# Fixing TensorE's order of products in an encoder block, gating by one Silu, and moving its transfers to another queue

## The chip, the cores and the metric

The kernel runs on one core of a Trainium2 chip. The metric is the device time of one execution in microseconds (us). The engines of a core run side by side, each with its own queue of instructions in a fixed order: TensorE (PE; its weight loads are listed apart as PEld), VectorE (DVE), ScalarE (ACT), GpSimd (POOL) and SyncE (SP). SP computes nothing here; it issues transfers. POOL issues transfers too. An instruction at the head of a queue that waits holds up everything behind it on that engine.

## The reference

One layer of a bidirectional encoder on 1024 positions of width 1024, in float32:

```python
proj = x @ w_in                      # 5920 columns, cut into the parts below
# attention: 3 groups of 4 heads, windows (128,1), (512,4), (2048,16) = (width, dilation)
s = q @ k * dh**-0.5 + bias;  e = exp(s - max(s));  o = (e @ v) / sum(e)
y_attn = sum over groups of softmax(log denominators) * o
# gated linear attention, forward and backward scan, 4 heads of 64 x 128
y_gla = rmsnorm(o_fwd + o_bwd) * gla_norm_g * silu(gout)
merged = sigmoid(gate_a) * (y_attn @ w_attn_branch) + sigmoid(gate_g) * (y_gla @ w_gla_branch)
x = layernorm(alpha * x + merged @ w_out)
x = layernorm(alpha * x + square(relu(x @ w_ff1 + b_ff1)) @ w_ff2 + b_ff2)
```

Here silu(g) is g times sigmoid(g). The change bears on the input projection, on `silu(gout)` and on the attention that runs beside the projection.

## The kernel before

**Products.** Each float32 operand is split in two halves, hi and lo (a cast on ACT, a subtraction on DVE; `halve`, line 152), and a product is made of three matmuls, hi by hi, hi by lo and lo by hi (`mm3`, line 98). A block product of four 128-row slices is thus 12 matmuls of 512 columns.

**The projection by seven products.** Two blocks of 128 columns of `w_in` are computed together by a scheme of the Strassen kind (`proj`, line 638). The weight is cut in quarters A11, A12, A22 and sums S1 to S4, and x in quarters B11 to B22 and sums T1 to T4. The text orders the products m1, m6, m2, m7, m5, m4, m3. After each comes a sum on DVE (`add`, line 632): after m6 the sum u2 is updated; after m7 the function `u3` reads bank W and u2; after m5 `c22` reads bank Z. Product m4 then accumulates *onto bank W*, so it cannot start before `u3` has read it, and m3 accumulates onto bank Z after `c22`. In the order of the text m5 stands between m7 and m4. For the first ten pairs after the first two, m1 and m2 were partly made earlier (`kept`), and five products remain: m6, m7, m5, m4, m3.

**Steps.** The projection is a list of 98 steps (list `steps`, loop at line 1151). Steps 0 to 9 finish the first two pairs, steps 10 to 19 are the products of the attention's values (`v_do`, line 1063, each 24 matmuls of 384 columns; prepared by `v_prep`), steps 20 to 69 ten pairs of five products, steps 70 to 97 four pairs of seven. A step's operands are prepared three steps ahead. Beside the steps run "units": from step 35 on the 24 attention tiles (`visit`, line 1092), with scores, exponentials, transposes and the products with the values; and from step 8 on eight pieces of the gating.

**What sets the order.** The order of the text is not the order of the queues. A planner simulates the program and, for each engine, may take a later instruction that it holds to be ready before an earlier one that it holds to be waiting. `tc.issue_after(i)`, and `behind(k)` that looks `i` up under the name k (line 635), forbid this: the instructions inside are queued after instruction i of the same engine. The matmuls of a projection product stand behind the name "small" only, the last attention matmul; those of the values' products stand behind nothing. Products may so be exchanged among themselves. The first matmul of an attention tile's products with the values stands behind "pe", the last product. SP's transfers of weights, stored blocks and parked sums are chained by the name "sp", and POOL's by "pool" (`pool_dma`, line 826), which makes the order of these queues that of the text.

**Gating.** `silu(h, hf)` (line 1012) loads a piece g of gout and a piece y of the linear attention's output (both SP, lines 1018 and 1019), makes the sigmoid of g on ACT (line 1023), two multiplications on DVE (lines 1025 and 1026) and stores y (SP, line 1027). Two sets of buffers serve in turn. The loads of piece i are placed at step 8 + 2i, its work at step 12 + 2i.

**Statistics of the attention.** Groups 1 and 2 store each tile's minima and denominators (`smdr`); `stats(g)` (line 991) fetches them, in two transfers by POOL, at visits 12 and 16.

**The end of the stage.** From step 92 on `fed` (line 1136) loads the gating's and the attention's results and splits them for the merge, two pieces a step, ahead of the preparation of the projection's own operands.

Of the kernel before, what the change touches and what calls it, by code (L numbers as in the profile page):

```python
# [12 lines left out]
AF = mybir.ActivationFunctionType  # L13
OP = mybir.AluOpType
# [34 lines left out]
def turns(tiles, n):  # L49

    count = itertools.count()
    return lambda: tiles[next(count) % n]
# [20 lines left out]
def build(tc, io):  # L73
    nc = tc.nc
    V, G, A, T, SP = nc.vector, nc.gpsimd, nc.scalar, nc.tensor, nc.sync
    P = Pools(tc)
    issued = {}
# [10 lines left out]
    def load_w(src, shape, raw=None):  # L88
        if raw is None:
            raw = wp.tile(shape, F32, tag="raw", bufs=2, name="raw")  # L90
            issued["raw"] = SP.dma_start(raw, src)
        hi = wp.tile(shape, F32R, tag="whi", bufs=4, name="whi")
        A.copy(hi, raw)
        lo = wp.tile(shape, F32R, tag="wlo", bufs=4, name="wlo")
        V.tensor_tensor(lo, raw, hi.bitcast(F32), op=OP.subtract)
        return hi, lo

    def mm3(ps, pairs, first=True, last=True, more=False):

        n = len(pairs)  # L100
        for i, (lh, ll, rh, rl) in enumerate(pairs):
            T.matmul(ps, lh, rh, start=first and i == 0, stop=False, skip_group_check=more)  # L102
            T.matmul(ps, lh, rl, start=False, stop=False, skip_group_check=more)  # L103
            issued["pe"] = T.matmul(ps, ll, rh, start=False, stop=last and i == n - 1, skip_group_check=more)  # L104
# [4 lines left out]
    spill = dr.tile([36, 128, S], F32, name="spill")  # L109
    yodr = dr.tile([4, 128, S], F32, name="yodr")  # L110
    ygdr = dr.tile([4, 128, S], F32, name="ygdr")
# [3 lines left out]
    smdr = dr.tile([2, S, 8], F32, name="smdr")  # L115
# [73 lines left out]
    for k in range(KT):  # L189
        n = {0: 1, 1: 1, 2: 2, 4: 2, 6: 2}.get(k)  # L190
# [11 lines left out]
        for nm, hf in (("q", 0), ("k", 0), ("q", 1), ("k", 1)):  # L202
            hi, lo = w0[nm]
            sl = slice(hf * 512, hf * 512 + 512)
# [117 lines left out]
    for i in range(2):  # L322
        sl = slice(i * 512, i * 512 + 512)
# [186 lines left out]
    def xside(nm, p, k):  # L510
        return XQ[nm][:, p, k] if nm in XQ else XQ[nm, k][:, p]
# [120 lines left out]
    def add(o, a, b):  # L632
        issued["add"] = V.tensor_tensor(o, a, b, op=OP.add)  # L633

    def behind(k):
        return tc.issue_after(issued[k].ins) if k in issued else nullcontext()

    def proj(blocks, r, ahead, banks, kept=None):

        st, c, ps = {}, {}, {}  # L640

        def mm(b, l, x, more=False):
            if not more:
                ps[b] = banks()
            l = l.rearrange("p h (k f) -> p h k f", f=128)
            with behind("small"):
                mm3(ps[b], [(l[:, 0, k], l[:, 1, k], xside(x, 0, k), xside(x, 1, k)) for k in range(4)], not more, True, more)

        def left(src):
# [47 lines left out]
        def m1():  # L697
            mm("X", st["A11"], "B11")
            c["u2"] = cu()
            A.copy(c["u2"], ps["X"])  # L700

        def m6():
            mm("Y", st["S2"], "T2")
            add(c["u2"], c["u2"], ps["Y"])
            if "W" in ps:
                u3()
                c22()
# [9 lines left out]
        def m2():  # L717
            mm("X", st["A12"], "B21", True)
            o = cr()
            A.copy(stored(o), nat(ps["X"]))  # L720
            put(0, 0, o)
# [54 lines left out]
    a, b = p0["steps"][1], p0["steps"][4]  # L776
    steps = [(a[0], b[1]), p0["steps"][3], (b[0], a[1]), *p0["steps"][5:]] + [p1["steps"][n] for n in (1, 3, 4, 5, 6)]
# [18 lines left out]
    def strip(g):  # L796
# [8 lines left out]
    aks, avs, es_, ets = ([ap_.tile([128, 2, 256], F32, name=f"{nm}{i}") for i in range(m)]  # L805
                          for nm, m in (("ak", 2), ("av", 3), ("e", 4), ("et", 3)))
# [4 lines left out]
    s12, fT = ap_.tile([128, 8, 2, 8], F32, name="s12"), ap_.tile([12, 128], F32, name="fT")  # L811
# [14 lines left out]
    def pool_dma(dst, src):  # L826
        with behind("pool"):
            issued["pool"] = G.dma_start(dst, src)
# [161 lines left out]

    def stats(g):
        for u in range(2):
            pool_dma(s12[:, 4 * u:4 * u + 4, g - 1],
                        smdr[g - 1, 512 * u:512 * u + 512].rearrange("(t p) w -> p t w", p=128))

    def quarter(n):
        u, q = n // 2, n % 2
# [8 lines left out]
    def flat(t):  # L1006
        return t.rearrange("p a b -> p (a b)")[:, 0:512]


    gating = turns([[flat(x) for x in y] for y in (es_[0:2] + ets[0:1], es_[2:4] + ets[1:2])], 2)  # L1010

    def silu(h, hf):
        sl = slice(hf * 512, hf * 512 + 512)
        b = {}

        def load():
            b["g"], b["y"], b["s"] = gating()
            SP.dma_start(b["g"], spill[4 + h, :, sl])
            SP.dma_start(b["y"], yodr[h, :, sl])

        def do():
            g, y, sg = b["g"], b["y"], b["s"]
            A.activation(sg, g, AF.Sigmoid)
            with tc.issue_after(issued["add"].ins):
                V.tensor_tensor(y, y, g, op=OP.mult)
                V.tensor_tensor(y, y, sg, op=OP.mult)
            SP.dma_start(ygdr[h, :, sl], y)
        return load, do

    vs = ap_.tile([128, 2, 768], F32, tag="strip1", name="vs")  # L1030
# [4 lines left out]
    def v_fetch(f, h, u):  # L1035
        vraw[f, h, u] = p_raw().bitcast(F32).rearrange("p a b -> p (a b)")[:, 0:768]
        with behind("sp"):
            issued["sp"] = SP.dma_start(vraw[f, h, u].rearrange("p (k f) -> p k f", k=2), io["wtv"][f, 2 * h + u])
# [24 lines left out]
    def v_do(n, u):  # L1063
        hi, lo = (x.rearrange("p (k f) -> p k f", k=2) for x in vside[n, u])
        nm = {5: "T1", 6: "T2", 7: "T3", 4: "T4", 3: "B22"}[n]
        for t in range(4):
            ts = slice(t * 128, t * 128 + 128)
            if u == 0:
                vps[n, t] = vps[7, t] if n == 4 else banks_of[0]()[:, 0:384]
            ps = vps[n, t]  # L1070
            fresh = u == 0 and n != 4
            mm3(ps, [(xside(nm, 0, 2 * u + j)[:, ts], xside(nm, 1, 2 * u + j)[:, ts], hi[:, j], lo[:, j])
                     for j in range(2)], fresh, u == 1, n == 4)
            if u == 0:
                continue
            if n == 5:
                A.copy(vx[t], ps)
                continue
            o = {6: vu[t], 4: vu[t], 3: vx[t]}[n] if n != 7 else cr()[:, 0:384]
            add(o, vx[t] if n == 7 else o, ps)  # L1080
            if n == 6:
                add(vx[t], vx[t], o)
                continue
            r, c = {7: (4, 1), 4: (0, 1), 3: (4, 0)}[n]
            with behind("sp"):
                issued["sp"] = SP.dma_start(vdr[(r + t) * 128:(r + t) * 128 + 128, c * 384:c * 384 + 384], o)
# [14 lines left out]
    units = {}  # L1101
    units[4] = [lambda: v_fetch(1, 0, 0), lambda: v_fetch(1, 1, 0)]
    units[6] = [v_kept]
    units[7] = [lambda: v_fetch(1, 0, 1), lambda: v_fetch(1, 1, 1)]
    for i, (n, u) in enumerate((n, u) for n in (5, 6, 7, 4, 3) for u in range(2)):
        units.setdefault(8 + i, []).append(lambda n=n, u=u: v_prep(n, u))
# [6 lines left out]
    n1 = len(steps) - 7  # L1113
    at = [2 * min(i, 8) + 1.75 * min(max(i - 8, 0), 8) for i in range(26)]
    for i in range(26):
        n = n0 + 5 + int(at[i] + max(i - 16, 0) * (n1 - 6 - n0 - at[-1]) / 9)
# [4 lines left out]
        if i in (16, 18, 20, 22):  # L1121
            units[n + 1].append(lambda i=i: quarter((i - 16) // 2))
    for i in range(8):
        for n, f in zip((8 + 2 * i, 12 + 2 * i), silu(i // 2, i % 2)):
            units.setdefault(n, []).append(f)
    units[n0].append(tiles[0][0]) if n0 in units else units.setdefault(n0, [tiles[0][0]])
    fed = []
# [23 lines left out]
    for i in range(len(steps)):  # L1151
        for u in units.get(i, ()):
            u()
        if i == n1:
            P.close("att")
            ya, yg = branches()
        elif i > n1:
            if i > n1 + 3 and len(wbt) < 2:
                wbt[len(wbt)] = load_w(io["wb"][len(wbt)], [128, 6, 128])
            fed.pop(0)()  # L1160
            fed.pop(0)()
        if i + 3 < len(steps):
            steps[i + 3][0]()
        for f in steps[i][1]:
            f()
    P.close("pre")
    P.close("cx")
    for n in ("av", "tr", "sc", "mm"):
# [58 lines left out]
    w = []  # L1227
# [53 lines left out]
    ps = [bank8() for _ in range(8)]  # L1281
# [42 lines left out]
    w = [load_w(io["wo"][1, k2], [128, 2, 512]) for k2 in range(4)]  # L1324
# [347 lines left out]
    steps = []  # L1672
# [290 lines left out]
def make(arrays):  # L1963
    import concourse.bacc as _bacc
    nc = _bacc.Bacc("TRN2", target_bir_lowering=False, num_devices=1, dynamic_dma_scratch_size=1024)
    io = {}
    for n, a in arrays.items():
        io[n] = nc.dram_tensor(f"in_{n}", a.shape, mybir.dt.from_np(a.dtype), kind="ExternalInput").ap()
    io["out"] = nc.dram_tensor("out_0", (S, D), F32, kind="ExternalOutput").ap()
    with tile.TileContext(nc, schedule_with_timeline_sim=True) as tc:  # L1970
        build(tc, io)
    return nc
# [8 lines left out]
```

## Time and profile before

| | |
|---|---|
| Median of three runs | 1379.49 us (1377.84 to 1380.35) |
| The profiled execution's own time | 1372.63 us |
| Its span, first to last instruction | 1370.8 us |
| Mean granted TensorE clock | 0.997 |
| DVE, ACT, POOL busy | 1029.1, 632.5, 113.4 us |
| Transfers, by SP's queue and by POOL's | 235.77 MB and 19.54 MB |

How to read it: a row of the timeline gives start, duration, engine, line, operation, the tile written and the tiles read, and in brackets the idle time of that engine just before and what ended it. SPq is SP's queue of transfers; its rows are the issuing alone. A row of the stretches gives for each engine the busy time and the number of instructions, then the granted TensorE clock, the share of the DMA engines' time in use, and GB/s. The tile names `mm`, `sc` and `tr` are banks of TensorE's results; `xT` is a sum T1 to T4 of x, `x` a quarter; `pwlo`, `pwhi` and `px` are buffers of a weight's halves, and `praw` and `pwhi` also take raw weights; `cu` is u2, `cr` a result that is stored; `e` and `et` are the attention's buffers, which the gating borrows.

### The profile page before, as it was taken

Reading aid. Unit: us, or ns where it says so; the run is one execution under the profiler, and the core shown is the slowest. Engines: PE = TensorE matmul, PEld = TensorE weight load, DVE = VectorE, ACT = ScalarE, POOL = GpSimd, SP = SyncE. Lnnn points to the kernel's source line nnn. Section 1 sums busy time; section 2 is a strip of 40 time slices with the busy share of each in tenths; the row PEclk is TensorE's granted clock in tenths of the full one; section 3 lists DMA queues with packets and bytes.
Section 4 is the critical chain, followed back from the end, with each engine's and each line's share of the span. In section 5 each row is a group of like instructions: output and inputs, shape, how many; then the busy total and the mean of one; then the engine's idle time right before and its main releaser. Section 6 shows DMA issues by size and latency. Waiting matters only on the chain.

```text
span 1370.8 us, 18987 instructions
## 1 busy us (share of the span) xinstructions
PE 1352.6 (99%) x6781; PEld 1124.4 (82%) x6781; DVE 1029.1 (75%) x1772; ACT 632.5 (46%) x1199; POOL 113.4 (8%) x173
## 2 busy tenths in 40 slices
PE   9999999998999999999999999999999999999998
PEld 7988898887777777788888888888888888888886
DVE  7377669777777678757667777877867897786988
ACT  5346656322444344455316655555557433333333
POOL 0000000001343533100001000000000000000002
PEclk9999999999999999999999999999999999999999
DMA  7225754776566677665835465656654955445313
GB/s 253 75 60 172 246 169 138 241 258 178 176 216 199 176 205 185 199 224 193 318 158 186 167 231 188 231 197 214 236 194 157 376 204 168 154 134 160 105 33 123
DMA packets 125857, 256.95 MB, mean 187 GB/s; under 512 B 34005, under 2 KB 43893, under 8 KB 125764
## 3 DMA queue, kind: packets, MB, share of 16 engines
q1 hardware_dynamic: 118388, 235.77, 52.2%
q0 software_dynamic: 6944, 19.54, 5.0%
q8 instruction: 53, 0.87, 0.3%
q10 hardware_dynamic: 432, 0.44, 0.1%
q14 instruction: 40, 0.33, 0.1%
HBM read 175.61 MB, written 81.14 MB: 187 GB/s over the span
## 4 chain that ended last, share of the span: by engine, by line
PE 90%; DVE 3%; DMA 2%; issue 2%; ACT 2%; POOL 1%; SPq 0%; ACTq 0%; POOLq 0%; DVEq 0%
PE ps L102 18%; PE ps L103 18%; PE ps L104 18%; PE mm L102 8%; PE mm L104 8%; PE mm L103 8%; PE sc L871 1%; PE tr L895 1%; PE avp L910 1%; PE sc L102 1%; PE sc L104 1%; PE sc L103 1%; ACT xr L1372 1%; DVE cr L633 0%; PE tr L102 0%
## 5 line engine op out<-in xcount | busy, mean ns | idle before, releaser
L1353 ACT CAST T<-hp 128x1024 fp32r<-128x1024 f32 x36 | 37.9, 1051 | 109.9 <-PE ps L103 70.4
L104 PE MATMUL ps<-B,B 128*128 128x512 f32 x160 | 62.3, 389 | 0.0
L103 PE MATMUL ps<-B,B 128*128 128x512 f32 x160 | 62.3, 389 | 0.0
L102 PE MATMUL ps<-B,B 128*128 128x512 f32 x160 | 61.0, 390 | 0.5 <-ACT B L1353 0.5
L883 ACT ACTIVATE e<-e,sm 128x256 f32<-128x256 f32 (+2 forms) x96 | 43.3, 452 | 36.7 <-DVE sm L877 29.0
L1859 POOL TENSOR_TENSOR mv<-mv,mhalf 128x1 f32<-128x1 f32 x8 | 7.0, 880 | 607.3 <-DVE mv L1858 605.8
L104 PE MATMUL ps<-B,T 128*128 128x512 f32 x144 | 56.1, 390 | 0.0
L104 PE MATMUL ps<-T,T 128*128 128x512 f32 x144 | 56.1, 389 | 0.0
L102 PE MATMUL ps<-T,T 128*128 128x512 f32 x144 | 56.1, 389 | 0.0
L103 PE MATMUL ps<-B,T 128*128 128x512 f32 x144 | 56.1, 389 | 0.0
L102 PE MATMUL ps<-B,T 128*128 128x512 f32 x144 | 56.1, 389 | 0.0
L103 PE MATMUL ps<-T,T 128*128 128x512 f32 x144 | 56.1, 389 | 0.0
L1354 DVE TENSOR_TENSOR T<-hp,T 128x1024 fp32r<-128x1024 f32 x36 | 44.0, 1222 | 15.3 <-ACT T L1353 13.6
L1754 DVE TENSOR_TENSOR acc<-ps,acc 128x512 f32<-128x512 f32 x68 | 45.6, 686 | 12.7 <-PE ps L104 12.2
L102 PE MATMUL mm<-x,whi 128*128 128x512 f32 x136 | 53.6, 404 | 0.5 <-ACT xb L460 0.4
L102 PE MATMUL mm<-xT,pwlo 128*128 128x512 f32 x120 | 48.8, 407 | 5.0 <-DVE cr L633 3.6
L103 PE MATMUL mm<-x,whi 128*128 128x512 f32 x136 | 53.7, 395 | 0.0
L104 PE MATMUL mm<-x,wlo 128*128 128x512 f32 x136 | 53.4, 394 | 0.0
L633 DVE TENSOR_TENSOR cr<-cu,mm 128x512 f32<-128x512 f32 x44 | 35.1, 798 | 20.6 <-PE mm L104 20.3
L102 PE MATMUL ps<-T,fraw 128*128 128x512 f32 x128 | 49.7, 390 | 0.4 <-ACT T L1353 0.4
L103 PE MATMUL ps<-T,fraw 128*128 128x512 f32 x128 | 49.9, 390 | 0.0
L104 PE MATMUL ps<-T,fraw 128*128 128x512 f32 x128 | 49.7, 390 | 0.0
(589 smaller groups left out, 4270.3 us busy)
## 6 DMA issues: line engine op xcount, KB each, us to landing
hdr<-c SPq DMA_DIRECT2D x112, 256.0 KB, 2.9
hp<-hdr SPq DMA_DIRECT2D x56, 512.0 KB, 3.7
spill<-cr SPq DMA_DIRECT2D x54, 256.0 KB, 3.7
praw<-in_wfm SPq DMA_DIRECT2D x16, 512.0 KB, 6.5
pwhi<-in_wfm SPq DMA_DIRECT2D x16, 512.0 KB, 4.9
gate<-spill SPq DMA_DIRECT2D x32, 256.0 KB, 3.4
wa<-in_w SPq DMA_DIRECT2D x16, 512.0 KB, 4.4
wb<-in_w SPq DMA_DIRECT2D x16, 512.0 KB, 6.7
```

Of the source, the lines that this page charges most:

```text
L102: T.matmul(ps, lh, rh, start=first and i == 0, stop=False, skip_group_check=more)
L103: T.matmul(ps, lh, rl, start=False, stop=False, skip_group_check=more)
L104: issued["pe"] = T.matmul(ps, ll, rh, start=False, stop=last and i == n - 1, skip_group_check=more)
L633: issued["add"] = V.tensor_tensor(o, a, b, op=OP.add)
L871: mm = T.matmul(sps[i][:, pr, 0:w], q[ps_, pr], k[ps_, pr, 0:w], start=True, stop=True)
L883: issued["exp"] = A.activation(e, e, AF.Exp, bias=sm[:, h:h + 1], scale=-1.0, accum_out=sm[:, 4 + h:5 + h])
L895: T.transpose(tp[0:hi - lo, pr, j], b["e"][i][:, pr, lo:hi], ident)
L910: return T.matmul(av[64 * i:64 * i + 64, pr], vv[:, h * 64:h * 64 + 64], b["et"][i][p0:p0 + vv.shape[0], pr, j], start=j == pr == 0, stop= ...
L1353: A.copy(o[:, 0], src)
L1354: V.tensor_tensor(o[:, 1], src, o[:, 0].bitcast(F32), op=OP.subtract)
L1372: A.activation(q[i][:, k], tp[:, k], AF.Identity, bias=cols[:, c + 8:c + 9], scale=cols[:, c:c + 1])
L1754: V.tensor_tensor(m, p, m, op=OP.add)
```

## The change

TensorE: from step 10 on every projection product, and every values' product, is queued behind the product before it in the text. Gating: one Silu on ACT and one multiplication on DVE in place of Sigmoid and two; its 24 transfers go by POOL in place of SP; three sets of two buffers in place of two sets of three; the loads are placed at step 6 + 2i. Statistics: the four transfers go by SP, in its chain, in place of POOL. End of the stage: for the steps 92 to 94 the pieces of `fed` come after the step's products, and from step 95 on after the preparation of the step three ahead.

```diff
-            with behind("small"):
+            with behind("pe" if "fixed" in issued else "none"), behind("small"):
                 mm3(ps[b], [(l[:, 0, k], l[:, 1, k], xside(x, 0, k), xside(x, 1, k)) for k in range(4)], not more, True, more)
...
     def stats(g):
         for u in range(2):
-            pool_dma(s12[:, 4 * u:4 * u + 4, g - 1],
-                        smdr[g - 1, 512 * u:512 * u + 512].rearrange("(t p) w -> p t w", p=128))
+            with behind("sp"):
+                issued["sp"] = SP.dma_start(s12[:, 4 * u:4 * u + 4, g - 1],
+                                            smdr[g - 1, 512 * u:512 * u + 512].rearrange("(t p) w -> p t w", p=128))
...
-    gating = turns([[flat(x) for x in y] for y in (es_[0:2] + ets[0:1], es_[2:4] + ets[1:2])], 2)
+    gating = turns([[flat(x) for x in y] for y in (es_[0:2], es_[2:4], ets[0:2])], 3)
...
         def load():
-            b["g"], b["y"], b["s"] = gating()
-            SP.dma_start(b["g"], spill[4 + h, :, sl])
-            SP.dma_start(b["y"], yodr[h, :, sl])
+            b["g"], b["y"] = gating()
+            pool_dma(b["g"], spill[4 + h, :, sl])
+            pool_dma(b["y"], yodr[h, :, sl])
 
         def do():
-            g, y, sg = b["g"], b["y"], b["s"]
-            A.activation(sg, g, AF.Sigmoid)
-            with tc.issue_after(issued["add"].ins):
+            g, y = b["g"], b["y"]
+            A.activation(g, g, AF.Silu)
+            with behind("add"):
                 V.tensor_tensor(y, y, g, op=OP.mult)
-                V.tensor_tensor(y, y, sg, op=OP.mult)
-            SP.dma_start(ygdr[h, :, sl], y)
+            pool_dma(ygdr[h, :, sl], y)
...
-            mm3(ps, [(xside(nm, 0, 2 * u + j)[:, ts], xside(nm, 1, 2 * u + j)[:, ts], hi[:, j], lo[:, j])
-                     for j in range(2)], fresh, u == 1, n == 4)
+            with behind("pe"):
+                mm3(ps, [(xside(nm, 0, 2 * u + j)[:, ts], xside(nm, 1, 2 * u + j)[:, ts], hi[:, j], lo[:, j])
+                         for j in range(2)], fresh, u == 1, n == 4)
...
+    units[10] = [lambda: issued.__setitem__("fixed", True)]
...
-        for n, f in zip((8 + 2 * i, 12 + 2 * i), silu(i // 2, i % 2)):
+        for n, f in zip((6 + 2 * i, 12 + 2 * i), silu(i // 2, i % 2)):
...
+        if i + 3 < len(steps):
+            steps[i + 3][0]()
+        if i > n1 + 3:
             fed.pop(0)()
             fed.pop(0)()
-        if i + 3 < len(steps):
-            steps[i + 3][0]()
         for f in steps[i][1]:
             f()
+        if n1 < i <= n1 + 3:
+            fed.pop(0)()
+            fed.pop(0)()
```

## The prediction

> **What bounds the kernel now.** First the page's busy times and its chain of waits, then the stretches of the projection stage, then the waits of TensorE.
>
> ```profile
> PE 1352.6 (99%) x6781; PEld 1124.4 (82%) x6781; DVE 1029.1 (75%) x1772; ACT 632.5 (46%) x1199; POOL 113.4 (8%) x173
> PE 90%; DVE 3%; DMA 2%; issue 2%; ACT 2%; POOL 1%; SPq 0%; ACTq 0%; POOLq 0%; DVEq 0%
> ```
> ```profile
> 254.10:295.86 41.76, 41.76 (x241) 41.60 (x240) 34.08 (x51) 13.72 (x21) 0.00 (x0) 1.00 0.84 287
> 295.86:341.86 46.00, 39.58 (x157) 31.27 (x157) 30.26 (x44) 9.63 (x16) 3.64 (x5) 0.93 0.58 171
> 341.86:570.00 228.14, 225.91 (x1377) 177.80 (x1378) 170.58 (x523) 98.63 (x303) 85.36 (x128) 1.00 0.66 193
> 570.00:592.00 22.00, 20.55 (x91) 16.68 (x91) 18.68 (x31) 13.86 (x21) 0.74 (x1) 1.00 0.75 251
> ```
> ```profile
> PE mm L102 <- DVE cr L633: 6.3, 2, 3.6
> PE sc L871 <- DMA ak<-spill: 1.5, 1, 1.5
> PE mm L102 <- ACT cr L720: 1.4, 1, 1.4
> ```
>
> TensorE sets the time: busy 99%, and 90% of the chain. The change takes no matmul away, so it can win only where TensorE stands still or runs slowly. The four stretches are the values' products, the projections of steps 20 to 34, those beside the attention, and the last pair. Only the second stands out: 46.00 us with 6.42 idle and a granted clock of 0.93. The others lose 0, 2.23 and 1.45. The waits say the same.
>
> The second stretch in the timeline, around its first halt:
>
> ```profile
> 288.21 0.69 DVE L683 TENSOR_TENSOR psum<-praw 128x512 f32<-128x512 f32 x1
> 290.62 0.69 DVE L154 TENSOR_TENSOR px<-psum,px 128x512 fp32r<-128x512 f32 x1
> 295.86 0.39 PE L102 MATMUL mm<-xT,px 128*128 128x512 f32 x1
> 299.98 0.39 SPq L1018 DMA_DIRECT2D e<-spill  x1
> 303.49 0.63 ACT L1023 ACTIVATE et<-e 128x512 f32<-128x512 f32 x1 [6.95 <-DMA e<-spill]
> 303.61 0.39 PE L103 MATMUL mm<-xT,pwlo 128*128 128x512 f32 x1
> 303.83 0.39 PE L104 MATMUL mm<-xT,pwlo 128*128 128x512 f32 x1
> 304.03 0.60 ACT L153 CAST pwlo<-pwhi 128x512 fp32r<-128x512 f32 x1
> 304.66 0.69 DVE L154 TENSOR_TENSOR pwlo<-pwhi,pwlo 128x512 fp32r<-128x512 f32 x1 [1.83 <-ACT pwlo L153]
> 305.87 1.06 DVE L633 TENSOR_TENSOR cr<-cu,mm 128x512 f32<-128x512 f32 x1
> 306.99 0.79 PE L102 MATMUL mm<-xT,pwhi 128*128 128x512 f32 x1 [2.77 <-DVE cr L633]
> 311.42 0.39 PE L102 MATMUL mm<-x,pwlo 128*128 128x512 f32 x1
> 308.00:310.00 2.00, 2.00 (x6) 1.60 (x5) 2.00 (x5) 0.62 (x1) 0.00 (x0) 0.50 0.44 131
> ```
>
> Line 683 makes S1 and px takes its halves, so the product at 295.86 is m5: the planner has put m5 ahead of m6 and m7. Nothing then stands between m7 and m4, and m4 must wait for `u3`, the sum at 305.87. That sum is late as well: ACT stood 6.95 us before the gating's sigmoid, whose load SP issued only at 299.98; the cast at 304.03 stood behind it, and DVE's subtraction at 304.66 behind the cast. So two causes meet, an exchanged order and a late gating piece.
>
> The second halt:
>
> ```profile
> 322.30 0.39 PE L104 MATMUL mm<-xT,pwlo 128*128 128x512 f32 x1
> 322.72 0.69 DVE L633 TENSOR_TENSOR cu<-cu,mm 128x512 f32<-128x512 f32 x1 [5.78 <-PE mm L104]
> 323.33 0.68 DVE L1025 TENSOR_TENSOR e<-e,e 128x512 f32<-128x512 f32 x1
> 325.13 1.06 DVE L633 TENSOR_TENSOR cr<-cu,mm 128x512 f32<-128x512 f32 x1
> 326.25 0.50 PE L102 MATMUL mm<-xT,pwlo 128*128 128x512 f32 x1 [3.57 <-DVE cr L633]
> 330.55 0.55 PE L102 MATMUL mm<-x,pwlo 128*128 128x512 f32 x1
> ```
>
> DVE had waited 5.78 us for TensorE when it updated u2, the sum after m6: here m6 came last of the three. Then a gating multiplication (323.33), two operations of the preparation and `u3` (325.13) had to pass before m4. TensorE and DVE waited for each other in turn.
>
> **The change part by part.** *Order.* Matmuls follow one another by 0.22 to 0.23 us (303.61 to 303.83), so a product of 12 takes 2.72. The first halt is 306.99 less the expected 304.06, 2.93 us; its m4 then lasts 311.42 - 306.99 = 4.43, 1.71 too long, at a clock of 0.50. The second is 326.25 - 322.53 = 3.72, and its m4 lasts 4.30, 1.58 too long. Together 9.94 us. Check: the stretch holds 13 products, 13 x 2.72 = 35.4 of 46.0, so 10.6 us is all that can go there. In the order of the text m5 stands between m7 and m4 and gives `u3` 2.72 us of cover. `u3` itself takes 1.06; the rest, 1.66, is two DVE operations of 0.69. With the gating's waits gone I take the cover to hold and count -9.9. If only one halt goes, -4.6 or -5.3; if the fixed order holds TensorE at a late operand that it stepped around before, the bound on that side is another halt of the kind, +5.3. For the 240 matmuls of the values' products there is nothing to win (idle 0.00).
>
> The rule of the Trainium skill that bears on the clock is in "TensorE: Matmul & The Clock Gate", Part 1: half rate comes after an idle window of about 3.4 us. By it the first halt, 2.77 us, would not surely have cost clock, and the sum would be 1.7 smaller; the row at 308.00 shows 0.50, and the measurement decides.
>
> *Gating.* Removed are eight multiplications on DVE; Silu takes Sigmoid's place:
>
> ```profile
> L1026 DVE TENSOR_TENSOR e<-e,et 128x512 f32<-128x512 f32 x8 | 5.5, 687 | 0.1
> SPq L1019 <- DMA ygdr<-e: 13.8, 6, 3.2
> L1023 ACT ACT_TABLE_LOAD x1 | 1.3, 1283 | 0.0
> e<-spill SPq DMA_DIRECT2D x8, 256.0 KB, 4.0
> ygdr<-e SPq DMA_DIRECT2D x8, 256.0 KB, 6.5
> ak<-spill POOLq DMA_DIRECT2D x10, 256.0 KB, 4.5
> ```
>
> 5.5 us of DVE go, beside TensorE's products: 0 by themselves, part of the slack above. No row shows Silu. Its nearest row is Sigmoid's, 0.63, and one table load of 1.3 stood before the first; Silu's load takes that place. Below, nothing can be won, since ACT idles 28 of the 41.8 us; above, a load at each of the eight pieces would be 10 us of ACT, spread over the same idle time. 0. SP's queue stood 13.8 us before the loads of y, until the set's last store had landed, with weights and stored blocks behind; that goes. POOL has no instruction at all in the values' stretch (x0) and takes 24 transfers, each some 0.73 to issue (row 448.44 below), 18 us over some 60. Behind its waiting stores now stand only later gating loads, and from step 30 the attention's first loads. Is it in time? Piece i+3 uses the set of piece i. After the multiplication the store must land (6.5) and the new y be loaded (4.5 by POOL's row of this size): about 12 us with two issues, against six steps, 16.3 us at 2.72, and more in the values' steps. It fits by some 4 us; 0.
>
> *Statistics.* The wait of 1.5 on ak has this past:
>
> ```profile
> POOL s L828 <- issue: 9.1, 4, 4.1
> 448.44 0.73 POOL L828 DMA_DIRECT2D ak<-spill  x1 [0.53 <-issue]
> 452.15 0.92 PE L871 MATMUL sc<-ak,aq 64*128 64x192 f32 x8 [1.49 <-DMA ak<-spill]
> ```
>
> POOL stood 9.1 us at four fetches, and the loads of q and k came behind. On SP they wait for `smdr` to land, and stored blocks and weights stand behind them; these have three steps of lead. SP's cost is bounded by the same 9.1 in all, four times 2.3, each less than 8 us of lead. -1.5.
>
> *Last pair.* ACT's copy that frees the bank for m5 stood behind a split of `fed`:
>
> ```profile
> 577.52 0.39 PE L102 MATMUL mm<-x,pwlo 128*128 128x512 f32 x1
> 581.15 0.62 ACT L153 CAST ya<-pre 128x512 fp32r<-128x512 f32 x1 [1.25 <-DMA pre<-yadr]
> 582.30 0.50 PE L102 MATMUL mm<-xT,pwlo 128*128 128x512 f32 x1 [1.45 <-ACT cr L720]
> ```
>
> m2 (577.52) came so late that only two matmuls of m7 stood between it and m5. In the text all of m7 does, 2.72 us, and the splits stand behind. -1.4; at worst the splits, now later, hold the merge's first product by as much.
>
> Sum: -9.9 - 1.5 - 1.4 = -12.8. I set against it +1.8 for waits that a new queue order brings somewhere: above one halt such as the 1.4 here and below the two whole halts, nearer the former, since the 228 us beside the attention, whose products are already held between attention matmuls, show only 2.2 of waiting. That gives -11.0: on the profiled execution 1372.63 - 11.0 = 1361.6, and on the median of the runs, which lies 6.9 above that execution, 1368.5. About 0.2%, 2.8 us, is what a measurement of this kernel can tell from none; the three runs lie 2.5 apart.
>
> **The rivals.** *One halt stays* (20%). `u3` needs m6's sum before it; where DVE has three operations of 0.69 ahead, 2.1 + 1.06 exceed the cover of 2.72. For it: DVE is busy 30.3 of 46.0 us there. Against: the cover is whole and eight operations go. Time: 1368.5 + 5.3 = 1373.8.
>
> *No change* (10%). The order does as it says, but the halts come back as waits for late operands: TensorE's fixed queue stops at one where it took another before. The sum of the halts is then as before, give or take the 1.5 of the statistics: 1379.
>
> *POOL's transfers are late* (10%), the other side. The gating's pieces of steps 20, 22, 24 and 26 hold ACT at the Silu, as ACT stood 6.95 before the sigmoid, and the casts behind it hold four projections, each at 2.93 + 1.71 = 4.6: 18.6 in place of the 12.8 taken away, 1379.5 + 5.8 = 1385. It decides where a piece takes over 16.3 us from the earlier multiplication to the loaded y. Against: some 12 by the rows.
> For it stands a page of the Trainium skill, "SBUF — State Buffer", SBUF: two separate sides: while VectorE holds the port pair that it shares with GpSimd, GpSimd cannot write the descriptors of its transfers, and one took 3.1 us in place of 0.62. By that price, as an estimate, the store and the load together would come 5 us later, past the point. The rows of before show POOL's loads at 4.5 against SP's 4.0 with DVE as busy, so I leave the case at its chance.
>
> **How the numbers follow.** The forecast has 60%; its own range runs from all of 12.8 and a little of the unexplained 0.7 of that stretch, 1366, to 1372. To hold 8 in 10 I go from 1364, where the runs lose more at the halts than the profiled execution did, to 1377, which takes in the rival of one halt and some 3 us of new waits beside it. Faster: 60 + 20 = 80%; within 0.2%: 10%; slower: 10%, that of the transfers.
>
> **What would show it.** Right: no wait of TensorE on `cr` (line 633) in steps 20 to 34, a clock of 1.00 there, the products of S2, S3, S1 in this order and the stretch near 36 us; no wait on ak after the statistics; m2 before m7 in the last pair; ACT never long before the Silu. Wrong: TensorE waiting for casts or subtractions (lines 153, 154) of the values' or the projections' operands; ACT or DVE waiting for a gating load by POOL; SP standing at the statistics with weights behind.

## The result and the profile after

The changed kernel takes 1362.22 us, the median of four runs (1360.89 to 1362.93), against 1378.66 us for the kernel before in the same comparison (four runs, 1377.25 to 1380.35). The ratio is 0.9879, with a 95% interval from 0.9862 to 0.9896: 16.4 us faster. The direction was forecast. The time is 6.3 us below the predicted 1368.5 and 1.8 below the low end of the range. The profiled execution, though, takes 1362.74 us, 9.9 less than that of before, where 11.0 were forecast. So the sum made on the trace was nearly right, and what failed lies between the trace and the median.

From the page of the changed kernel, the busy times:

```profile
PE 1349.8 (99%) x6781; PEld 1121.9 (82%) x6781; DVE 1025.2 (75%) x1764; ACT 630.9 (46%) x1199; POOL 122.6 (9%) x193
```

TensorE is still the bound, with the same 6781 matmuls. DVE has eight instructions fewer, POOL twenty more (24 of the gating added, four of the statistics gone).

The stretches of the changed kernel, cut at the same events as those of before (the values' products, the projections behind them, from the first scores on, the last pair; the cut ahead of the last pair is a round number in both):

```profile
254.79:297.14 42.35, 42.10 (x242) 41.48 (x240) 32.03 (x48) 13.88 (x22) 6.25 (x12) 1.00 0.86 298
297.14:335.73 38.59, 38.56 (x168) 31.35 (x168) 30.55 (x44) 10.06 (x17) 7.02 (x12) 1.00 0.68 200
335.73:558.00 222.27, 221.09 (x1362) 174.20 (x1362) 167.35 (x516) 96.86 (x302) 81.49 (x124) 1.00 0.66 196
558.00:578.87 20.87, 20.19 (x89) 16.35 (x88) 17.04 (x29) 12.35 (x21) 0.73 (x1) 1.00 0.71 239
```

The second stretch took 46.00 us for 157 matmuls at a clock of 0.93; now it takes 38.59 at 1.00, with 0.03 idle, and for 168 matmuls, since the first scores now stand one product later. With that product (2.72) taken off, the stretch is 35.9, where some 36 were forecast.

The waits of TensorE in the changed kernel, those of 0.6 us or more on operands and results of the projection's products (line, releaser, sum, times, longest):

```profile
PE tr L102 <- DVE cr L633: 0.8, 1, 0.8
...
PE mm L102 <- DVE cr L633: 0.7, 1, 0.7
PE mm L102 <- ACT x L153: 0.6, 1, 0.6
```

The halts on `cr` (6.3 in two), the wait on ak (1.5) and the wait on the copy of line 720 (1.4) are gone. What remains on `cr` is the wait of 0.8, which before has too, and one of 0.7 before the last product of the last pair.

The span adds up as follows. The columns are the lengths of the parts, in us, in the two profiled executions.

| from, to | before | after | difference |
|---|---|---|---|
| start of the span to the first values' product | 254.09 | 254.79 | +0.7 |
| values' products | 41.77 | 42.35 | +0.6 |
| projections behind them to the merge's first product | 294.73 | 281.73 | -13.0 |
| merge's first product to the first of the closing sums | 770.45 | 770.45 | 0.0 |
| closing sums to the end of the span | 9.76 | 11.58 | +1.8 |

The rows that bound the last two lines, first of before, then of the changed kernel (timeline of TensorE):

```profile
590.59 0.39 PE L102 MATMUL ps<-ya,whi 128*128 128x512 f32 x1
...
1361.04 2.41 PE L1876 MATMUL ps<-c,ones 1*128 1x512 f32 x6
1363.38 1.98 PE L1880 MATMUL ps<-acc,dg 128*128 128x512 f32 x4
```
```profile
578.87 0.39 PE L102 MATMUL ps<-ya,whi 128*128 128x512 f32 x1
...
1349.32 2.41 PE L1882 MATMUL ps<-c,ones 1*128 1x512 f32 x6
1351.66 3.45 PE L1886 MATMUL ps<-acc,dg 128*128 128x512 f32 x4
```

The halts and waits that the change takes away lie in the third line of the table, and there the forecast of -12.8 met -13.0, in which one new wait of 0.7 is already counted. The first line holds no product whose order the change fixes. In the last line the change touches nothing: 1.5 of the 1.8 are the same four matmuls, which take 3.45 in place of 1.98, because the granted clock falls in the last microseconds of the execution, here before these matmuls have ended:

```profile
1352.00:1356.00 4.00, 3.10 (x4) 0.67 (x2) 2.96 (x8) 1.45 (x3) 0.62 (x1) 0.57 0.17 66
```

In before the slice with the same matmuls, from 1364 to 1368, stood at 1.00.

### The profile page after: what moved, and what is told of

It reads as the page before. It is cut to its first block, busy times and chain, and to the rows that moved or that the text cites. A ratio compares the mean times of both kernels' runs of the same rounds, so it can differ in the third digit from the quotient of the medians.

```text
span 1360.9 us, 18993 instructions
## 1 busy us (share of the span) xinstructions
PE 1349.8 (99%) x6781; PEld 1121.9 (82%) x6781; DVE 1025.2 (75%) x1764; ACT 630.9 (46%) x1199; POOL 122.6 (9%) x193
## 4 chain that ended last, share of the span: by engine, by line
PE 92%; DMA 3%; DVE 2%; ACT 2%; SPq 1%; issue 1%; ACTq 0%; DVEq 0%
PE ps L102 18%; PE ps L103 18%; PE ps L104 18%; PE mm L102 9%; PE mm L104 9%; PE mm L103 9%; PE avp L910 1%; PE sc L871 1%; PE tr L895 1%; DMA xrh<-in_xT 1%; ACT xr L1378 1%; PE sc L104 1%; PE sc L102 1%; PE sc L103 1%; DMA pwhi<-in_wtv 0%
## 5 line engine op out<-in xcount | busy, mean ns | idle before, releaser
L1478 ACT ACTIVATE c<-c,cols 128x512 f32<-128x512 f32 x48 | 34.7, 725 | 30.2 <-DVE c L1539 13.7
```

Source lines behind the costliest of these rows:

```text
L1478: A.activation(q, src, AF.Relu, bias=cols[:, 2 * j + f:2 * j + f + 1])
```

## The experiments

Versions are named by their parts: the order of TensorE, the gating (Silu, one multiplication, three sets, loads two steps earlier, transfers by POOL), the statistics by SP, and the place of `fed`. Unless an edit says more, a version is the kernel before with the parts named, or the changed kernel with the parts taken back. Ratios are to the kernel before, run in the same comparison. All versions compute the whole output.

### The kernel before once more

No edit.

> The kernel before, unchanged, for a second profile of it on the chip of the comparisons. The timed runs of before lie 6.0 us above its profiled execution (1378.7 against 1372.6), those of the changed kernel do not (1362.2 against 1362.7). Theory 'halts vary': the missing 6 us lie in the steps 20 to 34, where the wait of TensorE on the sums grows from 6.3 us to about 10 and the time at half clock with it, and in no other stage. Rival 'everything is a little slower there': each of the stages is longer by 0.4%, the waits unchanged. Second rival: another wait, of a stage that the profile of before shows without one, appears in this execution.

Measured: 1376.75 us (ten runs, 1374.2 to 1380.2), ratio 1.0004 (0.9988 to 1.0020). Its profiled execution is 3.9 us longer than the one on which the prediction rests. The waits of TensorE in it, and then its stretches around the halts (the last three columns are the clock, the DMA share and GB/s):

```profile
PE mm L102 <- DVE cr L633: 6.7, 2, 3.6
PE sc L871 <- DMA ak<-spill: 1.8, 1, 1.8
PE mm L102 <- ACT cr L720: 1.3, 1, 1.3
```
```profile
308.00:312.00 4.00, 3.87 (x9) 3.10 (x10) 3.68 (x7) 1.02 (x2) 0.00 (x0) 0.50 0.40 111
312.00:316.00 4.00, 4.00 (x14) 3.11 (x14) 2.34 (x4) 0.73 (x2) 0.00 (x0) 0.71 0.98 290
452.00:456.00 4.00, 2.23 (x17) 1.58 (x16) 2.29 (x6) 0.62 (x1) 2.72 (x4) 0.78 0.63 191
```

The waits are nearly the same: 9.8 us in sum against 9.2. The time behind them is not: the slices of 4 us from 304 to 316 stand at 0.94, 0.50 and 0.71, where in the first execution they stood at 0.87, 0.70 and 1.00. Reckoned as time at 0.50 that is 8 x (0.06 + 0.50 + 0.29) = 6.8 us in place of 8 x (0.13 + 0.30) = 3.4. After the wait on ak, which cost no clock in the first execution, it is low as well. The stretch from the projections to the scores is 47.06 in place of 46.00, the one beside the attention 226.13 in place of 223.93 up to the same products. That is 3.3 of the 3.9. So between these two executions the halts hardly differ, but what they cost in clock does.

The runs point the same way. Over the four comparisons of this section before ran 49 times, from 1371.4 to 1381.4 us. The 12 runs with a mean granted clock of 0.997 or more (the execution on which the prediction rests had 0.997) have a median of 1373.7; the 23 from 0.994 to 0.996 have 1376.9, and the 14 at 0.993 or less have 1378.6.

### The order alone

```diff
+            with behind("pe" if "fixed" in issued else "none"), behind("small"):   # projections
...
+            with behind("pe"):                                                     # values
...
+    units[10] = [lambda: issued.__setitem__("fixed", True)]
```

> Only the fixed order of the projection's and the values' products; gating, statistics and the end of the stage as before. Theory 'order': the halts come from the exchanged products, and the gating's lateness counts only through them: no halt on the sums in steps 20 to 34, 1367 to 1370 us, 9 to 11 faster. Rival 'late gating': ACT still stands some 7 us before the sigmoid's load and holds the casts; at most one halt goes, 1373 to 1375.

Measured: 1369.0 us (five runs, 1368.23 to 1372.2), ratio 0.9946 (0.9925 to 0.9967). The second halt is gone, and the wait of line 720 with it; the first stays. Its timeline:

```profile
302.85 0.54 SPq L1018 DMA_DIRECT2D e<-spill  x1
306.41 0.39 PE L104 MATMUL mm<-xT,px 128*128 128x512 f32 x1
306.64 0.63 ACT L1023 ACTIVATE et<-e 128x512 f32<-128x512 f32 x1 [4.85 <-DMA e<-spill]
307.18 0.60 ACT L153 CAST pwlo<-psum 128x512 fp32r<-128x512 f32 x1
307.81 0.69 DVE L154 TENSOR_TENSOR pwlo<-psum,pwlo 128x512 fp32r<-128x512 f32 x1 [4.52 <-ACT pwlo L153]
308.42 1.06 DVE L633 TENSOR_TENSOR cr<-cu,mm 128x512 f32<-128x512 f32 x1
309.54 0.50 PE L102 MATMUL mm<-xT,pwhi 128*128 128x512 f32 x1 [2.74 <-DVE cr L633]
```

m5 (`px`, to 306.41) stands where the text has it, and still m4 waits 2.74 us. `u3` (308.42) is late for the other cause that the prediction named: ACT stood 4.85 us before the sigmoid for a load that SP issued at 302.85, and the cast and DVE's subtraction stood behind it in turn. The cover that m5 gives is used up by a gating piece that comes late. The order does what was said of it, and alone it is the rival "one halt stays".

### The gating alone

```diff
+    gating = turns([[flat(x) for x in y] for y in (es_[0:2], es_[2:4], ets[0:2])], 3)
...
+            pool_dma(b["g"], spill[4 + h, :, sl])     # and y, and the store
...
+            A.activation(g, g, AF.Silu)               # then one multiplication
...
+        for n, f in zip((6 + 2 * i, 12 + 2 * i), silu(i // 2, i % 2)):
```

> Only the gating: Silu, one multiplication, three sets, transfers by POOL, loads at step 6 + 2i; the planner may still exchange products. Theory 'order': m4 still comes right behind m7 or m6, and a halt of 1.5 to 3.6 us stays with its time at half clock: 1372 to 1376. Rival 'late gating': ACT no longer waits and the halts are gone: 1366 to 1369.

Measured: 1376.12 us (ten runs, 1372.44 to 1380.1), ratio 0.9993 (0.9976 to 1.0011): no difference. The wait of TensorE on ak, from the view of its waits, and the two halts in its timeline:

```profile
PE sc L871 <- DMA ak<-spill: 2.6, 1, 2.6
```
```profile
306.72 0.47 PE L102 MATMUL mm<-xT,pwhi 128*128 128x512 f32 x1 [1.25 <-DVE cr L633]
324.34 0.50 PE L102 MATMUL mm<-xT,pwlo 128*128 128x512 f32 x1 [3.56 <-DVE cr L633]
```

The first halt falls from 2.77 to 1.25, the second stays whole: there m6 was cut in two, two matmuls of it ahead of m7 and ten behind, so `u2` came late again: DVE took it up at 320.82, after waiting 6.42 us for TensorE. An earlier gating piece doesn't help against an exchanged order. That the median shows no gain at all has a second cause in this trace: from the projections to the first scores it is 3.3 us shorter than before (42.71 in place of 46.00), but from there to the last tile's values 5.1 longer (229.04 in place of 223.93), where the wait on ak has grown from 1.5 to 2.6 and is followed by 6.8 us at half clock.

### Order and gating, and then the statistics

The two parts above together; in the second version `stats` by SP as well.

```diff
+            with behind("sp"):
+                issued["sp"] = SP.dma_start(s12[:, 4 * u:4 * u + 4, g - 1],
...
```

> Order and gating together, statistics and the end of the stage as before. Both theories: no halt in steps 20 to 34; what is left to the changed kernel's 1362.2 us are the wait on ak (1.5) and that on the copy in the last pair (1.4): 1364 to 1366. If POOL, which keeps the statistics, delays the attention's loads more than before, the wait on ak is over 1.5.

> Order, gating and statistics; the end of the stage as before. Theory: the wait on ak (2.4 us in the profile with order and gating, with 4 us at half clock behind it) goes with the statistics, 1362.5 to 1364, and the last pair, whose m2 the order already puts before m7, keeps no wait on the copy. Rival 'the wait on ak comes from POOL's other work': it stays over 1 us, 1365 to 1366.

Measured: order and gating 1366.17 us (four runs, 1363.31 to 1367.39), ratio 0.9921 (0.9895 to 0.9948); with the statistics 1363.81 (four runs, 1359.33 to 1364.6), ratio 0.9899 (0.9878 to 0.9921), in another comparison. With order and gating both halts are gone. What is left is the wait on ak, and it costs clock; the row of the wait, then the stretches around it:

```profile
PE sc L871 <- DMA ak<-spill: 2.4, 1, 2.4
```
```profile
440.00:444.00 4.00, 1.65 (x17) 1.40 (x16) 2.39 (x5) 0.62 (x1) 2.34 (x5) 0.82 0.62 203
444.00:448.00 4.00, 4.00 (x18) 3.28 (x15) 1.80 (x9) 1.92 (x7) 2.06 (x3) 0.50 0.54 149
```

The wait on ak is 2.4 and 2.6 us in the two profiles in which POOL has both the gating and the statistics, against 1.5, 1.8 and 1.6 in the three in which SP has the gating; what makes the difference was not traced. With the statistics on SP no wait on ak is left. In the changed kernel the two fetches of a group are two issues of SP (timeline of the queue):

```profile
426.98 0.92 SPq L994 DMA_DIRECT2D s<-smdr  x2
```

0.92 us for both, where POOL had stood 9.1 us at four; the loads of q and k by POOL now come without a stop. The intervals of the two versions overlap, so the trace, not the medians, carries this step. The wait of line 720 was gone without the move of `fed`: the fixed order removes it, so that the move of `fed` by itself has nothing measurable left to win here.

### The gating's transfers by SP

The changed kernel with the gating's three transfers back on SP's queue. It was run in two comparisons.

```diff
-            pool_dma(b["g"], spill[4 + h, :, sl])
+            SP.dma_start(b["g"], spill[4 + h, :, sl])   # and y, and the store
...
```

> The changed kernel with the gating's 24 transfers left on SP; Silu, one multiplication, three sets and step 6 + 2i kept. Theory 'sets and lead': SP waits for the stores, but three sets and six steps are enough: no halt, 1362 to 1363. Rival 'the queue': weights and stored blocks stand behind the gating's waits, ACT waits 5 us or more before a Silu in steps 20 to 26, and a halt of 1 to 3 us is back, 1364 to 1368.

> The changed kernel once more, beside the next two on one chip. No halt of TensorE over 0.8 us and no time at half clock: 1361 to 1363, runs within some 2 us, against before's 7.

> The changed kernel with the gating's transfers on SP, again. Theory 'sets and lead, not the queue': equal to the changed kernel within 1 us or faster by 1 to 1.5, 1360 to 1362. Rival 'the queue matters': slower than it by 1 us or more.

Measured: by SP 1360.62 us (four runs, 1360.45 to 1362.67), ratio 0.9888 (0.9866 to 0.9909), and in the second comparison 1362.67 (six runs, 1360.42 to 1366.13), ratio 0.9912 (0.9897 to 0.9927), beside the changed kernel itself at 1362.04 (four runs, 1362.0 to 1362.09), ratio 0.9906 (0.9891 to 0.9921). The changed kernel's gain is 13.5 us in this comparison, since before stands at 1375.50 in it (eleven runs), while the changed kernel repeats its time to 0.2. The queue makes no difference that shows. In the first of the two profiles by SP, SP again stands before the loads of y for the stores to land, 9.8 us for one kind of buffer and 4.4 for the other, and ACT stands 35.3 us before the Silu (25.1 in the changed kernel), but the waits of TensorE are all 1.2 us or less. The runs of this version lie up to 5.7 us apart though its profiles show no halt, so a narrow spread is not a sure sign.

### The order fixed from the first step

The version before this, with the order fixed from step 0 in place of step 10.

```diff
-    units[10] = [lambda: issued.__setitem__("fixed", True)]
...
     fed = []
     wbt, pa = {}, {}
+    issued["fixed"] = True
```

> The same with the products' order fixed from step 0 in place of step 10. Theory 'an exchanged product is what makes TensorE wait for a sum': the wait of 0.8 us on the sum in step 9, which every profile so far has, goes as well: 0.5 to 1 faster than the kernel with the order from step 10, 1359.5 to 1361. Rival 'that wait is a late sum': it stays, or another comes, 0 to 2 slower, 1360.5 to 1363.

Measured: 1363.59 us (six runs, 1363.02 to 1369.0), ratio 0.9924 (0.9906 to 0.9942). One new wait of more than 1 us, between steps 0 and 10; its row in the timeline of TensorE, and the stretch around it:

```profile
237.28 0.50 PE L102 MATMUL sc<-xT,pwlo 128*128 128x512 f32 x1 [1.98 <-DVE cr L633]
```
```profile
236.00:240.00 4.00, 2.72 (x12) 2.26 (x13) 3.21 (x6) 2.33 (x3) 0.00 (x0) 1.00 0.17 66
```

Here the planner's exchange had covered a late sum, with a wait of 0.8 at another product, and the fixed order stops 1.98 at it. That is the mechanism of the rival "no change"; it exists, in steps that the change leaves alone. So the gain that the first expectation named did not come: the median is 0.9 above the same version fixed from step 10, within what the intervals leave open.

### Halts put in

The changed kernel with a chain of small copies on ACT (three, or seven) and a matmul that waits for them, ahead of m4 of one projection; they add work whose result nobody uses.

```diff
+            if kept == 0:
+                y = s12.rearrange("p a b c -> p (a b c)")
+                A.copy(y, ps["Z"][:, 0:128])
+                for _ in range(2):                    # 6 in the long one
+                    A.copy(y, y)
+                with behind("pe"):
+                    issued["pe"] = T.matmul(fillp[:, 0:128], y, ident, start=True, stop=True)
             mm("W", st["A22"], "T4", True)
```

> The changed kernel, with one halt of TensorE put in between m5 and m4 of the third pair (step 23): m4 stands behind a small matmul whose operand ACT copies three times in a row; nothing else in TensorE's order differs, and the copies are extra work without use. Theory 'a halt costs its length and, past some length, time at half clock': a halt of 1.3 to 1.6 us costs just that, 1363.5 to 1364, with no time at half clock. Rival 'a halt costs its length': the same here; the two part at the longer halt.

> The same with seven copies, a halt of 2.5 to 3.2 us. Theory 'a halt costs its length and time at half clock': 4.5 to 7 us over the changed kernel, 1367 to 1369, the runs spread over 3 us or more because the half clock lasts differently from run to run, and the mean granted clock falls by 0.001 to 0.004. Rival 'a halt costs its length, and the spread of before has another cause': 1365 to 1365.5, as narrow as the changed kernel's 2 us.

Measured: 1366.14 us (five runs, 1362.93 to 1366.2), ratio 0.9917 (0.9900 to 0.9933), and 1367.88 (five runs, 1367.28 to 1371.38), ratio 0.9940 (0.9923 to 0.9958). Both halts came out longer than meant, since ACT does casts between the copies; so the short one does not test that a halt of 1.3 to 1.6 us costs only itself. The short one, in the timeline of TensorE the halt, the first matmul of m4 and that of the product behind it, then the stretch with its clock; behind them the same of the long one:

```profile
307.87 0.49 PE L740 MATMUL avp<-ident,s 128*128 128x128 f32 x2 [2.23 <-ACT s L738]
308.11 0.48 PE L102 MATMUL mm<-xT,pwhi 128*128 128x512 f32 x1
312.53 0.39 PE L102 MATMUL mm<-x,pwlo 128*128 128x512 f32 x1
```
```profile
308.00:312.00 4.00, 4.00 (x13) 3.14 (x14) 1.59 (x3) 0.62 (x1) 0.00 (x0) 0.60 0.97 295
```
```profile
310.42 0.80 PE L740 MATMUL avp<-ident,s 128*128 128x128 f32 x2 [3.94 <-ACT s L738]
310.87 0.77 PE L102 MATMUL mm<-xT,pwhi 128*128 128x512 f32 x1
316.14 0.58 PE L102 MATMUL mm<-x,pwlo 128*128 128x512 f32 x1
```
```profile
312.00:316.00 4.00, 4.00 (x11) 3.13 (x10) 0.00 (x0) 0.00 (x0) 0.00 (x0) 0.50 0.24 97
```

After 2.23 us of halt m4 takes 312.53 - 308.11 = 4.42 in place of 2.72, 1.70 more; after 3.94 us it takes 5.27, 2.55 more. Read in slices of 0.1 us, the clock is at 0.50 for 3.4 us behind the short halt (from 308.8) and for 6.8 behind the long one (from 309.7): one and two periods of the kind that the last section describes. With the halts out of the changed kernel no such time is left in it: the slices of 4 us from 240 to 620 all stand at 0.995 or above. The long version has other late operands too (1.7 us on `cr`), so its 1371.38 in the profiled execution isn't the halt's alone.

### Two sets of buffers and the old lead

Order, statistics and `fed` of the change, Silu and one multiplication, but two sets of buffers, the loads at step 8 + 2i, and SP's queue.

```diff
-    gating = turns([[flat(x) for x in y] for y in (es_[0:2], es_[2:4], ets[0:2])], 3)
+    gating = turns([[flat(x) for x in y] for y in (es_[0:2], es_[2:4])], 2)
...
-        for n, f in zip((6 + 2 * i, 12 + 2 * i), silu(i // 2, i % 2)):
+        for n, f in zip((8 + 2 * i, 12 + 2 * i), silu(i // 2, i % 2)):
```

> Order, statistics, end of the stage, Silu and one multiplication; but the gating's transfers on SP, two sets of buffers and loads at step 8 + 2i, as before. Theory 'sets and lead': the pieces of steps 20 to 26 are late again, ACT stands 4 us or more before a Silu there and a halt of 1 to 3 us is back with its half clock: 1364 to 1368. Rival 'the operations': the multiplication taken off DVE and the shorter chain are what the order still lacked, no halt over 1 us, 1361 to 1363.

Measured: 1363.83 us (five runs, 1361.5 to 1366.07), ratio 0.9905 (0.9883 to 0.9927). On the median nothing can be told from the changed kernel. The profiled execution, the slowest of the five, has a halt again. First ACT's wait and SP's from the views of waits, then SP's issue of a weight and TensorE's halt from the timeline, then the stretches around it:

```profile
ACT pwlo L153 <- DMA praw<-in_wfm: 8.2, 1, 8.2
SPq L1020 <- DMA ygdr<-e: 16.5, 6, 3.8
```
```profile
310.25 1.18 SPq L660 DMA_DIRECT2D praw<-in_wfm  x2
321.60 0.50 PE L102 MATMUL mm<-xT,pwlo 128*128 128x512 f32 x1 [1.79 <-DVE cr L633]
```
```profile
320.00:324.00 4.00, 2.40 (x8) 1.97 (x9) 3.91 (x6) 0.99 (x2) 0.90 (x1) 0.87 0.41 129
324.00:328.00 4.00, 4.00 (x14) 3.14 (x13) 3.31 (x6) 1.16 (x2) 0.00 (x0) 0.71 0.91 270
```

SP, which again stands 16.5 us for stores to land, issues the weight at 310.25; in the changed kernel it does at 306.94. The nearer comparison, the two profiles with three sets and the gating on SP, has it at 307.32 and 306.31. ACT waits 8.2 us for the weight, DVE's subtraction behind ACT, and `u3` behind that. So in this execution the sets and the lead are what keeps a weight in time; on the median the gain is there without them. How much of the gating's part is Silu and the multiplication, and how much the lead, was not separated further.

## Why the prediction was right, and where it was wrong

*The two halts, one from an exchanged order and a late piece.* Right, and the runs show that it takes both parts: order alone leaves one halt of 2.74, gating alone leaves halts of 1.25 and 3.56 and no gain in the median, both together leave none. In the profiled executions the way from the projections to the last tile's values, in which the halts and the wait on ak lay, went from 269.93 to 257.65 us, 12.3 less, where -9.9 and -1.5 make 11.4.

*The step that failed* is the carry-over to the median, "and on the median of the runs, which lies 6.9 above that execution, 1368.5". The 6.9 were taken as a fixed offset of the kernel. What the runs show in its place is a cost of the halts: the clock terms, 1.71 and 1.58 and nothing behind the wait on ak, were read in one execution at the fast edge of the runs, and in the second profiled one the same halts cost more clock (0.50 and 0.71 over 8 us, and 0.78 behind ak), two more periods at half clock (the last section), which lose 3.4 us. With the halts the offset left too: the changed kernel's median lies 0.5 below its profiled execution, and 0.04 above it when run again. The second profile accounts for 3.3 of the 6.9; that the rest is of the same kind is argued from the granted clocks of the 49 runs, since there is no profile of a run at 1379 us, and the three runs behind the 1379.49 have no clock on record. 6.9 + 0.5 too much, less the 1.1 that the trace's own sum was short (11.0 against 9.9), is the error of 6.3. The range's low end allowed for this with 4.5 us, "where the runs lose more at the halts than the profiled execution did", and that was too little.

*Statistics, -1.5.* Right in the trace: the wait on ak is gone as soon as SP does the fetches, and not before. It was sized without clock; where the wait is 1.8 to 2.6 us it costs clock too.

*Last pair, -1.4.* Half of it. The order holds, and the copy of line 720 is in time. But m3, the last product, then waits 0.7 us for a sum of DVE (`c22`), which stands behind two splits of `ya` that waited for ACT (timeline of DVE, changed kernel):

```profile
573.97 1.36 DVE L154 TENSOR_TENSOR ya<-pre,ya 128x512 fp32r<-128x512 f32 x2 [2.18 <-ACT ya L153]
575.24 0.68 DVE L633 TENSOR_TENSOR cr<-cr,mm 128x512 f32<-128x512 f32 x1
```

That is the prediction's "at worst the splits, now later", one product earlier than it said. From the last tile's values to the merge 24.80 us became 24.08.

*+1.8 for new waits.* 1.3 came ahead of the projections (0.6 is the wait on `x`, line 153; 0.2 is a wait in the values' stretch; the rest has no row) and 0.7 in the last pair: 2.0, about the size taken, and in part by luck: the way to the first values' product, on which the change fixes no order, took 254.79 us in this execution and 254.22 in the second of the changed kernel, in which the wait in the last pair is 0.3. The 1.8 us at the end of the span came on top and were nobody's; they are the clock of the last microseconds. Without them the profiled execution would be 11.7 us below before's, where 11.0 were forecast.

*The rivals.* "One halt stays" did not come, for the reason that the order-alone run shows: the piece was no longer late. POOL's transfers being late did not come either, though the loads moved the way of that rival. The changed kernel's issues of transfers, with the time to landing last:

```profile
e<-spill POOLq DMA_DIRECT2D x6, 256.0 KB, 5.7
e<-yodr POOLq DMA_DIRECT2D x6, 256.0 KB, 5.2
ygdr<-e POOLq DMA_DIRECT2D x6, 256.0 KB, 5.2
```

The loads land in 5.2 to 5.7 us where SP's took 4.0 and 4.4, the store in 5.2 where SP's took 6.5. Each issue took POOL 0.55 us, with DVE busy 32.03 of 42.35 us in the values' stretch. The starvation of which the Trainium skill speaks in "SBUF — State Buffer", SBUF: two separate sides (a transfer of 3.1 us in place of 0.62 beside a copy by VectorE), does not show in these rows.

*"ACT never long before the Silu"* was wrong as a sign. The waits of ACT from 240 to 345 us in the changed kernel:

```profile
ACT e L1024 <- DMA e<-spill: 18.5, 4, 7.5
ACT et L1024 <- DMA et<-spill: 6.6, 1, 6.6
```

ACT still stands 25.1 us there in the changed kernel, against 28.0 before. It no longer holds TensorE, which has 0.03 us of idle time in the stretch. What the order-alone run shows is the case that counts: a cast that TensorE needs next, standing behind such a wait.

## What to carry to other kernels

A halt of TensorE of about two microseconds is to be priced as the halt and the half-clock time behind it, here nothing, 1.7 or 3.4 us by where the halt fell, so that this part differs from run to run; where the profiled execution is a cheap one, as here, taking the halts out brings the median further down than it says. Before an offset between a profiled execution and the median is carried over to a changed kernel, ask whether the change removes what makes it. Where a late transfer and an exchanged order meet in a halt, mend both: here the order alone left one halt of two, and the earlier transfer alone shortened one and left the other.

## What the runs showed of the hardware

Whether a halt costs clock did not follow its length alone. Halts up to 1.6 us left the granted clock at 1.00 (1.25, 1.45, 1.49, 1.6); those from 2.23 us on all brought it down (2.23, 2.35, 2.6, 2.74, 2.77, 3.56, 3.57, 3.94), to 0.50 where a slice lay wholly in it. Between them it went both ways: 1.79 and 1.8 cost clock, 1.98 did not.

The traces show what decides. Read in slices of 0.1 us, the clock between 240 and 620 us stands at 0.50 for some 3.4 or 6.8 us at a time and for no other length. Within one execution these stretches begin at multiples of 3.413 us from one another: in the first profile of before at 307.0, 327.4 and 1368.5 us, which is 6 and 311 such periods apart. So the clock changes at the ends of periods that run on through the execution. Cut into these periods, counted back from a fall of the clock near the end of each execution, the traces give for the halts (idle share: TensorE's idle time in the period that holds most of the halt):

| halt, us | version | idle share of the period | clock in the next period |
|---|---|---|---|
| 1.98 | order fixed from step 0 | 36% | 1.00 |
| 1.49 | before | 43% | 1.00 |
| 1.6 | order alone | 48% | 1.00 |
| 2.6 | gating alone | 51% | 0.50 |
| 1.8 | before once more | 52% | 0.50 |
| 1.79 | two sets, old lead | 53% | 0.50 |
| 2.23 | short halt | 65% | 0.50 |
| 2.77 | before, first halt | 80% | 0.50 |
| 3.94 | long halt | 94% | 0.50 |

In all 14 profiles, from 30 us on to the last microseconds, 12 periods at full clock have an idle share of 51% or more, and half clock follows every one of them; the others have 48% or less, and it follows none. The halt of 1.98 us lay across the end of a period, 0.74 us before it and 1.24 behind; the one of 1.79 lay in one period. A period at half clock loses 1.7 us of a busy TensorE. A second one followed where TensorE still stood still for 14 to 24% of the first (four times, and once at 15% it did not), none where it was busy (eleven times at 0 or 1%). Where a period begins differs from execution to execution, and so the same halt costs one period in one and two in another, as the first halt of before did.

The Trainium skill, "TensorE: Matmul & The Clock Gate", Part 1, gives an idle window of about 3.4 us before the clock falls, and calls the window free-running. The length and the free running are what these traces show; that the whole window must be idle is not, since an idle share of 51% was enough.
